# Late first reads, six first raw tiles and two closing banks on ScalarE in a two-layer decoder trunk

## The chip, the cores and the metric

The kernel runs on one core of a Trainium2 chip, as one program. The metric is the device time of one execution in microseconds (us). The core has TensorE (PE in the profile; PEld is its weight load), VectorE (DVE), ScalarE (ACT), GpSimd (POOL) and SyncE (SP), each with its own in-order queue. DMAs are issued here from SP's queue (q1 of the profile) and from POOL's (q0) and share 16 DMA engines.

## The reference: what is computed

Two layers over x (1, 256, 2048) in float32. The weights come from memory once per execution, in float32.

```python
h = rms_norm(x, attn_norm)
proj = einsum('bsd,de->bse', h, w_in)           # 2048 x 6160
# gated linear attention heads, stick-breaking heads, each normalised -> mixed
x = x + einsum('bse,ed->bsd', mixed, w_o)       # 2048 x 2048
hm = rms_norm(x, mlp_norm)
up = square(relu(einsum('bsd,df->bsf', hm, w_up)))   # 2048 x 8192
x = x + einsum('bsf,fd->bsd', up, w_down)       # 8192 x 2048
```

## The kernel before, in words

**Products.** Each float32 operand is split in a high part (rounded to TensorE's float32r) and a low part (the rest), and a product is three matmuls: high·high, high·low, low·high (L1224, L1227, L1228). For a weight tile, ScalarE makes the high part `whi` (L1091) and VectorE the low part `wlo` (L1095) from the loaded tile `raw`. `raw` tiles of 1 MB are loaded over SP's queue (L1016) into three slots (`RAWS`).

**Big units.** The large products are cut in units of 256 rows by 1024 columns over 2048 inputs: `up` and `down`, in four quarters of two units each, `o`, and, one layer ahead, `iv`, `ik` and `iq` of the next layer's input projection. A unit goes over eight pairs of 256 inputs, cut in 2 x 2 blocks. A fast pair takes seven block products instead of eight: VectorE forms four sums of weight blocks (`ts` and in place, L871) and four of operand blocks (`forms`, L464 to L467), and the products go to PSUM banks named m1 to m8. Banks m2, m4, m3, m8 are the four output blocks; m1, m6, m5, m7 are sums that the unit's closing distributes over them. Pairs that aren't fast go to the four output banks alone. Two pairs of each unit ("added") get their weights by POOL's queue instead: `chi` is loaded (L1052), ScalarE writes its negative into `dlo` (L1056), and a second, adding load (L1059) turns that into the low part. There are three `chi` tiles; in the first scope each of the first three loads comes behind a one-column ScalarE write into its tile (`held_tile`, L1045), which reads `ident`.

**Closing a unit.** `up_tail` (L1338) and `seeded_tail` (L1288) first copy m1 (ScalarE), then VectorE forms dw = m6 - m1 and adds: m5 + dw, m7 + dw, m5 + that; when an output bank is done, VectorE adds it, one addition for each of the four. A bank is free for the next unit when its last reader is done. Units that follow an `up` unit turn its output by TensorE transposes into m5 and m7 behind their first step, and into m1 and m6 behind their second (`turn`, L1384); units behind `o`, and (`down`, 3, 1) and `iv` in layer 0, do so with the residual.

**Order.** `Plan` takes each piece of work with an engine, an estimated length and what it depends on, simulates the engines, and writes the order of TensorE, VectorE and ScalarE out by hand (`manual_schedule`); of the ready pieces the one due first goes first. A unit's order of pairs stands in lists (`EACH`, `FEWER`, `LATER`, `O0`, `O1`, `OWN`). Every scope of units opens with five prelude pieces of 12 matmuls each, which stand for the unit that is still running. GpSimd's and SP's queues are ordered by the compiler, in which earlier lines go first among what is ready.

**Scopes.** The program opens with one plain unit (columns of `w_in`, lines L607 to L628, whose output is `acc`) while x is loaded, turned (L503) and split (L513, L519) and its squares summed (L560). Then come `iv`, `ik`, `iq` of layer 0 in the first planned scope; layer 0's attention; its planned scope (the gate unit, `o`, `up`, `down`, and layer 1's `iv`, `ik`, `iq`); layer 1's attention; and its planned scope, which ends the program with (`down`, 3, 1) and the store of x. L917 copies the plain unit's `acc` out. Between attention and planned scopes PSUM is laid out anew: attention has two `acc` tiles of two banks, then four single banks (L242); a planned scope has eight single banks in an order of their first use (L250):

```python
open_scope("psum", acc=2, ps=4)
order = (1, 6, 5, 7) if first else (5, 7, 1, 6)
unused.update((m, new_bank(m)) for m in (*order, 2, 4, 3, 8))
```

Of the kernel before, what the change touches and what calls it, by code (L numbers as in the profile page):

```python
# [14 lines left out]
ALU = mybir.AluOpType  # L15
# [7 lines left out]
EACH = [7, 7, 5, 2, 5, 5, 1, 1, 5, 4, 1, 1, 3, 3, 3, 3, 4, 6, 6, 2, 6, 6, 0, 0], FAST, (2, 4)  # L23
FEWER = [0, 0, 3, 2, 3, 3, 2, 3, 1, 1, 1, 7, 7, 1, 6, 6, 4, 6, 4, 6, 5, 5], (1, 3, 6), (2, 4)
LATER = [0, 0, 4, 1, 1, 1, 1, 3, 3, 4, 6, 6, 3, 6, 3, 6, 2, 5, 5, 5, 5, 2, 7, 7], FAST, (2, 4)
FAST_OF = {"sxh": (0, 1, 3, 5, 6), "sx": FAST}
TWO_WAYS = (("sxh", 0),)
O0 = [6, 6, 7, 4, 5, 4, 0, 0, 1, 0, 7, 0, 1, 1, 1, 5, 2, 2, 2, 2, 3, 3], (0, 1, 2), (5, 7)
O1 = [5, 7, 7, 0, 0, 0, 1, 0, 6, 1, 1, 2, 1, 2, 2, 2, 5, 3, 6, 3, 4, 4], (0, 1, 2), (5, 6)
SEEDED = (("down", 0), ("down", 1), ("o", 1))  # L30
SPARE = ()
OWN = {
    ("up", 0): ([4, 0, 0, 0, 0, 1, 1, 2, 1, 1, 6, 6, 2, 6, 6, 5, 5, 5, 5, 4, 3, 3, 3, 3, 7, 7], (0, 1, 3, 5, 6), (2, 4)),
    ("up", 0, 0): ([0, 0, 1, 1, 1, 4, 4, 1, 3, 3, 3, 6, 6, 3, 2, 6, 6, 5, 5, 5, 5, 2, 7, 7], FAST, (2, 4)),
    ("up", 1): ([0, 0, 3, 3, 3, 3, 2, 1, 1, 1, 2, 1, 5, 5, 5, 4, 6, 5, 6, 6, 6, 7, 4, 7], FAST, (2, 4)),
    ("down", 0): ([0, 0, 3, 3, 1, 2, 3, 3, 1, 1, 5, 1, 4, 5, 5, 5, 2, 6, 6, 6, 6, 7, 7, 4], FAST, (2, 4)),
    ("down", 1): ([0, 0, 5, 5, 4, 5, 5, 6, 6, 6, 4, 6, 3, 3, 3, 1, 2, 3, 1, 1, 1, 2, 7, 7], FAST, (2, 4)),
}
CAST, AHEAD_BY = 3, 1
RING, LOWS, ADDS, RAWS = 5, 4, 2, 3  # L40
# [21 lines left out]
class Plan:  # L62
# [8 lines left out]
    GAP = 0.06  # L71

# [18 lines left out]
    def run(self):  # L91
# [32 lines left out]
        while events:  # L124
# [9 lines left out]
            for e in free:  # L134
# [38 lines left out]
def trunk_kernel(  # L173
# [275 lines left out]
    def forms(op, i, t, tag):  # L449
# [9 lines left out]
        def sums():  # L459
            a11, a21, a12, a22 = (t[:, k, r * P : (r + 1) * P] for k in range(2) for r in range(2))  # L460
            n = 4 if keep else 3
            e.append(tmp("t2", [P, 512], bufs=T2)[:, : n * P].rearrange("p (k c) -> p k c", c=P))
            s = e[0][:, 3, :] if keep else a21
            nc.vector.tensor_tensor(e[0][:, 2, :], a21, a11, ALU.subtract)  # L464
            nc.vector.tensor_tensor(s, a21, a22, ALU.subtract)
            nc.vector.tensor_tensor(e[0][:, 0, :], a11, s, ALU.subtract)
            nc.vector.tensor_tensor(e[0][:, 1, :], a12, e[0][:, 0, :], ALU.subtract)  # L467
# [387 lines left out]
    def ordered(l, units, hT, rst, ug, gates_t, mixed=None, ons=None):  # L855
# [4 lines left out]
        open_scope("sbuf", mlp=1)  # L860
        hm = Operand()
# [4 lines left out]
        MM, TR, V2, V1, A2, A1 = 0.2268, 0.109, 1.15, 0.62, 1.06, 0.60  # L866
# [84 lines left out]
        def made(f, got, tag_fast, first):  # L951
# [3 lines left out]
            def part(k):  # L955
                if not box:
                    box.extend(f())
                box[k]()
# [44 lines left out]
        def load(u, i):  # L1003
# [4 lines left out]
            def fn():  # L1008
                if x % RAWS >= 3:
                    box.append(tmp("raw2", [P, 2, 1024], bufs=RAWS - 3))  # L1010
# [9 lines left out]
            if x >= RAWS:  # L1020
                piece.after = raws[x - RAWS]
# [13 lines left out]
        def rounded(u, j, s):  # L1035
# [9 lines left out]
            def held_tile():  # L1045
                box["h"] = tmp("chi", [P, 2, 512], F32R, bufs=CAST)
                nc.scalar.activation(box["h"][:, 0, :1], ident[:, :1], AF.Copy)
# [15 lines left out]
            if l < 0 and len(chi) < CAST:  # L1063
                first = add("ACT", 0.2, held_tile, before[0])
# [223 lines left out]
        def seeded_tail(u):  # L1288
# [18 lines left out]
            def sums(p):  # L1307
# [7 lines left out]
                d = vector(x22, bk(5), dw, b, p[5], seeds[8])  # L1315
                free.update({1: [c], 6: [w], 5: [a, d], 7: [b]})
# [615 lines left out]
```

## Time and profile before

| what | value |
|---|---|
| median of three runs | 2134.3 us (2134.24 to 2135.91) |
| profiled execution | 2134.41 us, span 2132.7 us |
| TensorE / VectorE / ScalarE / GpSimd busy | 99% / 90% / 68% / 13% |
| mean granted clock of TensorE | 0.999 |
| moved by DMA | 497.14 MB, mean 233 GB/s |
| first planned scope | 38.3 to 164.9 us |
| planned scope of layer 0 | 296.0 to 1199.8 us |
| planned scope of layer 1 | 1352.0 us to the end |

The three scope rows are the starts of the first product into a named bank and of the first that is none. A timeline row has start, length, engine, line, operation, tiles written<-read, shapes, count, and in brackets the engine's idle time before it with what ended that. Matmul lengths overlap: dense matmuls of 512 columns start every 0.227 us, and a gap in the starts is a stall. VectorE's lengths overlap a little too.

### The profile page before, as it was taken

What the parts mean: (1) busy time and instruction counts of PE and PEld (TensorE: products, weight loads), DVE (VectorE), ACT (ScalarE), POOL (GpSimd) and SP (SyncE); (2) the same over time, 40 slices, a digit from 0 to 9 for tenths busy, and PEclk for the clock granted to TensorE, in tenths of its full rate; (3) what the DMA queues carried; (4) which work ended last, traced back from release to release, by engine and by line L of the source; (5) the groups of instructions that cost most, each with busy time, mean ns of one, the idle gap of its engine ahead of it and who ended that gap; (6) DMA issues with size and microseconds to landing.
All of it is one profiled execution on the core that took longest, in us unless ns stands there. A gap on an engine that the chain in (4) does not pass through costs nothing.

```text
span 2132.7 us, 28217 instructions
## 1 busy us (share of the span) xinstructions
PE 2120.0 (99%) x10064; PEld 1763.6 (83%) x10064; DVE 1909.1 (90%) x2578; ACT 1452.1 (68%) x1940; POOL 276.4 (13%) x394
## 2 busy tenths in 40 slices
PE   8999999999999999999999999999999999999999
PEld 7888888888888888888888988888888888888887
DVE  5978779999999999999988896799999999999997
ACT  6657667676677677667766575677776776676774
POOL 1110001111111111111111100011112111111110
PEclk9999999999999999999999999999999999999999
DMA  8975358788988988988888644678889788889886
GB/s 257 259 227 174 115 176 242 223 255 243 271 245 244 268 245 245 283 244 234 250 261 245 192 138 138 213 217 244 264 241 272 234 262 256 240 246 273 242 245 200
DMA packets 157617, 497.14 MB, mean 233 GB/s; under 512 B 10682, under 2 KB 19458, under 8 KB 157476
## 3 DMA queue, kind: packets, MB, share of 16 engines
q1 hardware_dynamic: 100900, 319.16, 42.0%
q0 software_dynamic: 56576, 176.18, 36.9%
q8 instruction: 79, 1.29, 0.2%
q14 instruction: 62, 0.51, 0.1%
HBM read 493.20 MB, written 2.10 MB: 232 GB/s over the span
## 4 chain that ended last, share of the span: by engine, by line
PE 94%; DVE 3%; DMA 2%; ACT 1%; issue 1%; SPq 0%; ACTq 0%; DVEq 0%
PE acc L626 3%; PE acc L628 3%; PE acc L627 3%; DVE wlo L1095 1%; DMA xb<-in_x_dram 1%; DMA raw<-in_w_up_dram 1%; DMA raw<-in_w_in_dram 1%; PE ps L1869 0%; PE ps L1862 0%; DVE wlo L609 0%; PE ps L737 0%; PE ps L1819 0%; DVE ts L871 0%; PE ps L791 0%; PE ps L755 0%
## 5 line engine op out<-in xcount | busy, mean ns | idle before, releaser
L1095 DVE TENSOR_TENSOR wlo<-raw,whi 128x1024 fp32r<-128x1024 f32 (+1 forms) x689 | 744.0, 1089 | 86.2 <-ACT whi L1091 39.8
L1091 ACT ACTIVATE whi<-raw 128x1024 fp32r<-128x1024 f32 (+1 forms) x689 | 644.7, 950 | 185.8 <-DVE raw L871 67.6
L1056 ACT ACTIVATE dlo<-chi 128x1024 fp32r<-128x1024 f32 x168 | 177.6, 1057 | 117.7 <-DMA chi<-in_w_o_dram 5.1
L1091 ACT ACTIVATE whi<-ts 128x1024 fp32r<-128x1024 f32 x169 | 179.0, 1059 | 89.9 <-DVE ts L871 42.2
L871 DVE TENSOR_TENSOR ts<-raw 128x1024 f32<-128x1024 f32 x169 | 206.1, 1220 | 6.3 <-DMA raw<-in_w_o_dram 2.4
L1095 DVE TENSOR_TENSOR wlo<-ts,whi 128x1024 fp32r<-128x1024 f32 x169 | 206.1, 1220 | 4.1 <-ACT whi L1091 4.1
L626 PE MATMUL acc<-whi,act 128*128 128x512 f32 (+2 forms) x384 | 141.7, 369 | 1.6 <-ACT whi L607 1.6
L627 PE MATMUL acc<-wlo,act 128*128 128x512 f32 (+2 forms) x384 | 137.1, 357 | 0.2 <-DVE wlo L609 0.2
L628 PE MATMUL acc<-whi,act 128*128 128x512 f32 (+2 forms) x384 | 137.3, 358 | 0.0
L607 ACT ACTIVATE whi<-raw 128x1024 fp32r<-128x1024 f32 (+2 forms) x98 | 88.3, 906 | 69.2 <-PE acc L628 62.4
L609 DVE TENSOR_TENSOR wlo<-raw,whi 128x1024 fp32r<-128x1024 f32 (+2 forms) x98 | 100.3, 1030 | 32.5 <-ACT whi L607 32.3
L871 DVE TENSOR_TENSOR raw<-raw 128x512 f32<-128x512 f32 x169 | 116.2, 688 | 2.3
L871 DVE TENSOR_TENSOR raw<-ts,raw 128x512 f32<-128x512 f32 x169 | 115.8, 685 | 0.6
L1052 POOL DMA_DIRECT2D chi<-in_w_up_dram x64 | 38.0, 594 | 557.9 <-PE m__2856_13480 L1228 30.1
L1052 POOL DMA_DIRECT2D chi<-in_w_down_dram x64 | 38.8, 606 | 498.5 <-PE m__3324_15675 L1228 27.5
L1376 ACT ACTIVATE act<-act,st 128x512 f32<-128x512 f32 x88 | 60.2, 715 | 54.9 <-DVE act L871 54.9
L626 PEld LDWEIGHTS acc<-whi,act 128*128 128x128 f32 x384 | 72.6, 189 | 14.1 <-issue 3.4
L628 PEld LDWEIGHTS acc<-whi,act 128*128 128x128 f32 x384 | 72.7, 189 | 10.6
L627 PEld LDWEIGHTS acc<-wlo,act 128*128 128x128 f32 x384 | 72.8, 190 | 9.4 <-DVE wlo L609 0.5
L1059 POOL DMA_DIRECT2D dlo<-in_w_down_dram x64 | 60.1, 940 | 51.6 <-ACT dlo L1056 48.1
L1059 POOL DMA_DIRECT2D dlo<-in_w_up_dram x64 | 58.3, 912 | 55.9 <-ACT dlo L1056 53.6
L488 DVE TENSOR_TENSOR act<-t,act 128x512 fp32r<-128x512 f32 x92 | 62.7, 685 | 0.0
(4307 smaller groups left out, 5756.4 us busy)
## 6 DMA issues: line engine op xcount, KB each, us to landing
raw<-in_w_up_dram SPq DMA_DIRECT2D x96, 1024.0 KB, 7.4
raw<-in_w_down_dram SPq DMA_DIRECT2D x96, 1024.0 KB, 7.7
raw<-in_w_in_dram SPq DMA_DIRECT2D x72, 1024.0 KB, 5.7
chi<-in_w_up_dram POOLq DMA_DIRECT2D x64, 512.0 KB, 5.6
dlo<-in_w_up_dram POOLq DMA_DIRECT2D x64, 512.0 KB, 8.5
chi<-in_w_down_dram POOLq DMA_DIRECT2D x64, 512.0 KB, 5.6
dlo<-in_w_down_dram POOLq DMA_DIRECT2D x64, 512.0 KB, 8.5
raw<-in_w_o_dram SPq DMA_DIRECT2D x24, 1024.0 KB, 7.5
```

The lines of the kernel that those rows point to most:

```text
L488: nc.vector.tensor_tensor(d[:, :, 1, :], src, f32(d[:, :, 0, :]), ALU.subtract)
L607: newest["hi"] = nc.scalar.activation(h, r, AF.Copy).ins
L609: newest["lo"] = nc.vector.tensor_tensor(lo[:, q : q + step, :width], r, f32(h), ALU.subtract).ins
L626: nc.tensor.matmul(o, xh[:, sl], whi[:, j, :width], start=first, stop=False)
L627: nc.tensor.matmul(o, xh[:, sl], wlo[:, j, :width], start=False, stop=False)
L628: st["mm"] = nc.tensor.matmul(o, xl[:, sl], whi[:, j, :width], start=False, stop=last).ins
L871: nc.vector.tensor_tensor(dst, a, b, op)
L1052: nc.gpsimd.dma_start(flat("h"), src)
L1056: nc.scalar.activation(box["l"], f32(box["h"]), AF.Copy, scale=-1.0)
L1059: nc.gpsimd.dma_start(flat("l"), src, accum_op=ALU.add)
L1091: nc.scalar.activation(box["h"][:, :n], src(), AF.Copy)
L1095: nc.vector.tensor_tensor(box["l"][:, :n], src(), f32(box["h"][:, :n]), ALU.subtract)
```

## The change

It has three parts.

1. `held_tile` reads the low part of the last operand pair of x instead of `ident`, and doesn't wait for a prelude piece any more in the plan.
2. The first scope has six raw tiles instead of three; the three new ones are `raw2` tiles of the scope's own pool. The planner counts 0.12 us between two VectorE pieces of which one needs the other, the four sums of `forms` become four pieces, and estimated lengths of VectorE pieces are adjusted. One kept operand of the MLP moves to the pool of activations (`SPARE`).
3. In `up_tail` and `seeded_tail`, ScalarE copies banks m4 and m8 into the output block, and VectorE adds from there. m5's second addition moves behind the copy of m8, and dw is kept until both last additions are done.

The orders of the pairs are new in nearly all lists; how often each pair stands in a list, and which are fast or added, is as before.

```diff
-EACH = [7, 7, 5, 2, 5, 5, 1, 1, 5, 4, 1, 1, 3, 3, 3, 3, 4, 6, 6, 2, 6, 6, 0, 0], FAST, (2, 4)
+EACH = [0, 0, 1, 1, 1, 2, 7, 3, 3, 3, 3, 2, 5, 5, 5, 5, 4, 1, 6, 6, 6, 4, 6, 7], FAST, (2, 4)
...
-SPARE = ()
+SPARE = ("sxh",)
...
+FIRST_RAWS = 6
...
+    SAME = {"DVE": 0.12}
...
-                        at[u], free[e] + p.lag + (0.0 if u.engine == e else self.GAP)
+                        at[u], free[e] + p.lag + (self.SAME.get(e, 0.0) if u.engine == e else self.GAP)
...
+        slots = RAWS if l >= 0 else FIRST_RAWS
...
-        MM, TR, V2, V1, A2, A1 = 0.2268, 0.109, 1.15, 0.62, 1.06, 0.60
+        MM, TR, V2, V1, VS, A2, A1 = 0.2268, 0.109, 1.14, 0.61, 0.21, 1.06, 0.60
...
-                e = add("DVE", 1.25, lambda: part(0), first, take=1, sure=1 + got)
+                for k in range(4):
+                    kw = {} if k else dict(take=1, sure=1 + got)
+                    e = add("DVE", VS, lambda k=k: part(0, k), e, **kw)
...
-                nc.scalar.activation(box["h"][:, 0, :1], ident[:, :1], AF.Copy)
+                nc.scalar.activation(box["h"][:, 0, :1], f32(hT.t[7][:, 1, 1, :1]), AF.Copy)
...
-                first = add("ACT", 0.2, held_tile, before[0])
+                first = add("ACT", 0.2, held_tile)
...
-                b = vector(y(0, 1), bk(7), lambda: box["w"], w, a, p[7])
-                b.give = 1
-                d = vector(y(1, 1), bk(5), y(0, 1), b, p[5])
-                free.update({1: [c], 6: [w], 5: [a, d], 7: [b]})
-                box["s"] = (c, b, a, d)
+                b = vector(lambda: box["w"], bk(7), lambda: box["w"], w, a, p[7])
+                free.update({1: [c], 6: [w], 5: [a], 7: [b]})
+                box["s"] = (w, b, a, b)
...
+                    before = p[m]
+                    if tt:
+                        free[m] = before = [add(
+                            "ACT", A1,
+                            lambda m=m, h=h: nc.scalar.activation(
+                                box[h][:, 1, :], banks[m], AF.Copy
+                            ),
+                            before, box["c"],
+                        )]
+                    if m == 8:
+                        before = vector(y(1, 1), bk(5), y(1, 1), before, p[5])
+                        free[5] = free[5] + [before]
```

`seeded_tail` has the same edit with the residual's blocks in place of y.

More of the change, by code (lines that the diff above doesn't have):

```diff
@@ L1019, in load @@
             piece = add("SP", 2.9, fn, lag=LAND)
-            if x >= RAWS:
-                piece.after = raws[x - RAWS]
+            if x >= slots:
+                piece.after = raws[x - slots]
             raws.append(readers)
```

86 lines of the change are left out of this document (51 added, 35 removed).

## The prediction

> **What bounds the kernel now.** I read the page's busy shares, then the table by stretches, then the timelines of the stretches where TensorE is not dense.
>
> ```profile
> span 2132.7 us, 28217 instructions
> PE 2120.0 (99%) x10064; PEld 1763.6 (83%) x10064; DVE 1909.1 (90%) x2578; ACT 1452.1 (68%) x1940; POOL 276.4 (13%) x394
> ...
> 10.00:15.00 5.00, 4.51 (x12) 3.26 (x12) 2.77 (x5) 1.62 (x4) 0.00 (x0) 0.67 1.08 401
> 500.00:600.00 100.00, 100.00 (x442) 82.78 (x441) 94.66 (x115) 65.47 (x74) 17.20 (x22) 1.00 0.91 260
> 1900.00:2000.00 100.00, 100.00 (x443) 82.84 (x442) 91.92 (x108) 64.44 (x72) 16.91 (x22) 1.00 0.95 273
> ```
>
> In the last three rows the columns are the stretch, then busy time of PE, PEld, DVE, ACT and POOL, the granted clock, the DMA share and GB/s. In the big units TensorE has no gap (100.00 of 100), VectorE 5 to 8% idle, ScalarE 35%. The orders of the steps are permuted, but how many fast pairs, added pairs and products a unit has is unchanged, so TensorE's work is too. Inside the big units there is nothing to win; what the change moves lies at the opening, where scopes meet, and at the end.
>
> The profiled execution took 2134.4 us (its span and 1.7 around it), the three timed runs have their median at 2134.3: one number for this purpose. The sum is made on 2134.4.
>
> **Held reads, the opening.** The three first `chi` loads wait for a tiny ScalarE write that today needs only `ident`.
>
> ```profile
> 2.63 1.77 POOL L1052 DMA_DIRECT2D chi<-in_w_in_dram x3 [1.24 <-ACT chi L1047]
> ...
> q1 hardware_dynamic: 1048, 1.95, 58.2%
> q0 software_dynamic: 432, 1.57, 42.9%
> ...
> DMA packets 2173, 4.63 MB, mean 386 GB/s; under 512 B 131, under 2 KB 131, under 8 KB 2172
> ...
> 6.32 1.57 ACT L513 ACTIVATE act<-ps,gcol_a 128x256 fp32r<-128x256 f32 x4 [3.83 <-DVE gcol_a L345]
> 9.58 0.63 ACT L607 ACTIVATE whi<-raw 128x512 fp32r<-128x512 f32 x1 [1.69 <-DMA raw<-in_w_in_dram]
> ...
> 10.26 0.51 PE L626 MATMUL acc<-whi,act 128*128 128x512 f32 x1 [1.56 <-ACT whi L607]
> 16.05 1.09 PE L503 MATMUL ps<-ident,xb 128*128 128x128 f32 x8 [0.68 <-DMA xb<-in_x_dram]
> 20.11 1.09 PE L503 MATMUL ps<-ident,xb 128*128 128x128 f32 x8 [0.23 <-DMA xb<-in_x_dram]
> 20.96 0.47 PE L626 MATMUL acc<-whi,act 128*128 128x512 f32 x1
> ```
>
> The two queue rows are of 4 to 15 us: 1.57 MB of `chi` (q0) beside 1.95 MB of x and opening weights (q1), while ScalarE and TensorE wait for exactly those (rows of 9.58, 16.05, 20.11). The next row is 15 to 27 us, 386 GB/s without `chi`: 1.57 MB cost 4.1 us there. Without them the first weights find ScalarE free at 7.9, so the first product starts near 8.4 instead of 10.3; the first twelve products then go at VectorE's pace (four `wlo` of 0.69) to 11.5, the next x is turned by 12.4, and ScalarE (four copies, 1.6; two `whi`, 1.9) and VectorE (1.2) allow the second group near 16.2 instead of 20.96. The half clock of 10 to 15 us (0.67) follows the gap before 10.26 and should go with it; that is in the 16.2. Bounds: 1.9 (first product alone) to 5.0; I take **-4.7**. From 20 us on TensorE is dense, so the gain lasts to the unit's end (38.5, now 33.8).
>
> **Held reads, the scope behind.** This is the step that I expect to spoil it.
>
> ```profile
> 28.22 1.66 DVE L519 SCALAR_TENSOR_TENSOR act<-ps,gcol_a,act 128x256 fp32r<-128x256 f32 x4 [0.72 <-ACT act L513]
> 28.70:34.30 5.60, 5.60 (x27) 4.62 (x26) 4.61 (x10) 5.60 (x14) 0.00 (x0) 1.00 0.60 192
> 33.70 0.28 ACT L560 ACTIVATION_READ_ACCUMULATOR t<-xb 128x1 f32 x1
> 33.79 1.13 ACT L1091 ACTIVATE whi<-raw 128x1024 fp32r<-128x1024 f32 x1
> 38.49 0.60 ACT L917 ACTIVATE act<-acc 128x512 f32<-128x512 f32 x1 [3.57 <-PE acc L628]
> 38.99 1.05 ACT L1056 ACTIVATE dlo<-chi 128x1024 fp32r<-128x1024 f32 x1
> 40.41 1.06 ACT L1091 ACTIVATE whi<-raw 128x1024 fp32r<-128x1024 f32 x1
> ...
> 41.52 0.49 PE L1224 MATMUL m__82_434<-whi,act 128*128 128x512 f32 x1 [0.35 <-ACT whi L1091]
> 42.78 0.50 PE L1227 MATMUL m__82_434<-wlo,act 128*128 128x512 f32 x1 [0.77 <-DVE wlo L1095]
> ...
> chi<-in_w_in_dram POOLq DMA_DIRECT2D x11, 512.0 KB, 7.5
> ```
>
> ScalarE's order in this scope is written out by the planner. Today a held write waits for the first prelude piece (12 products, 2.7), so by the planner's clock `chi` lands at 11.1, after the first `whi` is ready at 9.96 (2.9 issue, 7.0 landing, 0.06): the order is `whi`, L917, `dlo`, and the rows show it. With that dependence gone the held writes stand at 0, the first `chi` lands at 8.32 and the second at 9.32, so ScalarE's order becomes held, `dlo`, `dlo`, `whi`, L917. ScalarE is in order: no `whi` before two `chi` have landed. But now `chi` is issued only after the last operand's low part (L519, 29.9) and, I think, behind ScalarE's own backlog (5.60 of 5.60 us busy from 28.7 to 34.3): the `whi` of 33.79 stood behind it too. Shifted by 4.7 that is 29.3, with the three writes 29.7. Landing takes 7.5 (the row of 0 to 130 us), the second 1 to 2 later: 37 to 39; one `dlo` and one `whi` of 0.95 each and the `wlo` of 1.14 give 40.3 to 42.2 for the first complete product, where TensorE is free at 33.8. Before, the scope started at 38.3 and lost 1.65 (0.51 and 1.03 by the starts ahead of the rows of 41.52 and 42.78, 0.11 behind): 39.9 in effect. So this stage ends 0.4 to 2.3 later than before, 1.0 the likeliest, and TensorE has idled over 4 us. The gap of 1.56 before 10.26 was followed by a granted clock of 0.67 over 5 us, 1.65 us lost; after a longer gap I add 1.6 (0 to 3.4). Stage sum **+2.6** (bounds +0.4 and +5.7), the opening's gain included.
>
> [...]
>
> **Six raw tiles, ScalarE copies: what they take away.**
>
> ```profile
> 123.47 1.22 DVE L871 TENSOR_TENSOR ts<-raw 128x1024 f32<-128x1024 f32 x1 [0.58 <-DMA raw<-in_w_in_dram]
> 124.62 0.68 DVE L871 TENSOR_TENSOR act<-m__157_811,act 128x512 f32<-128x512 f32 x1
> ...
> 125.36 0.50 PE L1224 MATMUL m__229_1148<-whi,act 128*128 128x512 f32 x1 [1.07 <-DVE act L871]
> ```
>
> VectorE waits for a raw tile, the closing addition of bank 4 stands behind it, and TensorE waits for that bank: 1.34 us by the starts. With three more tiles the raw lands earlier, and bank 4 is freed by ScalarE. I take **-1.3** (0 to -1.3).
>
> **ScalarE copies: what they add.** Per big unit two copies of 0.60 (row of 158.33 below), some 40 units, 48 us on an engine with 680 idle; VectorE keeps eight operations a unit. But bank 5 now gets its last reader behind the copy of bank 8, the unit's last product.
>
> ```profile
> 158.33 0.60 ACT L1347 ACTIVATE act<-m__246_1226 128x512 f32<-128x512 f32 x1 [3.64 <-PE m__246_1226 L1228]
> ...
> 162.18 0.69 DVE L871 TENSOR_TENSOR act<-m__241_1210,act 128x512 f32<-128x512 f32 x1
> 165.13 0.69 DVE L871 TENSOR_TENSOR act<-m__234_1171,act 128x512 f32<-128x512 f32 x1 [0.20 <-PE m__234_1171 L1228]
> ...
> 164.71 0.39 PE L1228 MATMUL m__234_1171<-whi,act 128*128 128x512 f32 x1
> 164.93 0.28 PE L626 MATMUL acc<-whi,act 128*128 128x272 f32 x1
> ```
>
> Where a scope ends, attention's first `acc` opens in the first two banks of the new pool, where m5 and m7 lay (`order`, L252). Today m5's last read is at 162.18, long before TensorE goes on at 164.93. After: the product ends at 165.10, copy to 165.74, addition of bank 5 from 165.80 to 166.49, TensorE at 166.55: 1.6 us of stall at the least, 2.9 behind one other ScalarE and one VectorE operation of 0.65. I take 1.9, twice (scope before layer 0, end of layer 0): **+3.8** (0 to 5.8; 0 if the placing is otherwise). Elsewhere bank 5 is next needed by the transposes 2.72 us (12 products) behind the unit's end: covered while both queues together hold under 1.1 us.
>
> The end of the kernel:
>
> ```profile
> 2120.58 0.69 DVE L871 TENSOR_TENSOR xb<-m__4033_18993,t 128x512 f32<-128x512 f32 x1
> 2121.30 0.69 DVE L871 TENSOR_TENSOR t<-m__4034_18997,t 128x512 f32<-128x512 f32 x1
> ...
> 2128.62 0.69 DVE L871 TENSOR_TENSOR xb<-m__4024_18956,xb 128x512 f32<-128x512 f32 x1 [0.67 <-PE m__4024_18956 L1228]
> ```
>
> Behind the last product stands one addition, then the store. After: a copy of 0.60, a hand-over of 0.06 and a second, dependent addition 0.72 behind the first (spacing of the rows of 2120.58 and 2121.30): **+1.4**, with nothing to hide it (1.3 to 1.5).
>
> [...]
>
> **Dependent steps counted, split sums, one tile from the act pool.** The same instructions, re-ordered; TensorE is dense over them, so nothing to gain. If VectorE, 92 to 95% busy in the rows above, came late with operands, TensorE would wait: 0 to +3, I take 0.
>
> **Sum:** 2134.4 + 2.6 - 1.3 + 3.8 + 1.4 = 2140.9, forecast 2141.
>
> **Rivals.**
> 1. *The held writes come early.* If ScalarE has one idle slot after 25.2 (29.9 less 4.7), the writes slip in ahead of the backlog and `chi` is issued 4 us sooner: landed at 33 and 35, first product complete at 37. Against 39.9 that is -3 instead of +2.6, 2135.3. For it: the three extra raw loads have no tile to wait for and may overtake the opening's last weights, which gives ScalarE such a slot. Against: 28.7 to 34.3 is dense today.
> 2. *Faster.* As in 1, and attention's first product doesn't wait for bank 5: 2134.4 - 3 (or -4.7, with the start's stall as before) - 1.3 + 1.4 gives 2131.5 or 2129.8, and 2129.5 with a little more than my take of the opening. For it only that the placing of banks is read from the code, not from a row. Against it: the end costs 1.4 in any case.
> 3. *Bank 5 late inside the layers.* About 20 places (up to up, up to down, o to up) need it 2.72 us behind a unit's end; the bare path is 1.6. From 1.1 us of queueing on it costs; at 0.3 us each, 6 us: 2147. Against: the addition of 165.13 starts 0.03 behind its product (164.71 and 0.39 long), so queues can be kept short there.
>
> **How the numbers follow.** The forecast 0.47, held writes early 0.30, faster 0.12, bank 5 late 0.11. A measurement here tells about 0.2%, 4.3 us, from no change. The forecast's own range is 2137 to 2144: slower in 0.37 of its 0.47. Rival 1 (2131 to 2138) is nearly all no change, 0.26, with 0.01 faster and 0.03 slower; rival 2 faster; rival 3 slower in 0.10. Faster 0.13, same 0.37, slower 0.50. Eight in ten reach from 2130, most of rival 2 left out, to 2147, half of rival 3.
>
> **What would show it.** No q0 traffic before 20 us, granted clock 1.00 in 10 to 15, opening unit over near 34 (opening). ScalarE with two L1056-type copies ahead of the first L1091-type one, TensorE idle over 4 us behind the opening unit, waiting for `whi` (scope). Attention's first product 1.6 to 2.9 behind the last product of bank 8, twice, released by VectorE (bank 5). A ScalarE copy and two additions behind the last product (end). No wait near 124. Wrong if ScalarE issues the held writes before its squares, or if the first `acc` follows without a gap; a dense TensorE in the big units that is not dense any more would be a cost that I priced at nothing.

## The result and the profile after

The changed kernel takes 2146.5 us (median of 4 runs, 2144.4 to 2151.9) against 2134.3 (2134.2 to 2135.9): ratio 1.0062 with the interval 1.0050 to 1.0074. It is slower by 12.3 us, about twice the 6.7 that I had forecast: near the upper edge of the wide range (2130 to 2147), and outside the forecast's own (2137 to 2144). Its profiled execution is its longest: 2151.9 us, span 2150.2.

The page after, its first rows:

```profile
span 2150.2 us, 28296 instructions
PE 2121.5 (99%) x10064; PEld 1765.5 (82%) x10064; DVE 1902.3 (88%) x2578; ACT 1490.5 (69%) x2020; POOL 274.5 (13%) x394
```

80 ScalarE instructions more, TensorE's and VectorE's counts the same. The table by stretches after (columns as in the prediction: stretch, busy time of PE, PEld, DVE, ACT, POOL, granted clock, DMA share, GB/s):

```profile
8.00:15.00 7.00, 6.38 (x31) 5.04 (x32) 4.99 (x12) 5.44 (x12) 0.00 (x0) 1.00 1.05 396
33.10:36.40 3.30, 0.59 (x3) 0.16 (x1) 0.00 (x0) 0.00 (x0) 0.00 (x0) 1.00 1.06 408
36.50:46.60 10.10, 4.19 (x9) 3.00 (x10) 4.68 (x6) 7.50 (x9) 1.77 (x2) 0.50 0.99 238
132.00:136.00 4.00, 4.00 (x12) 3.12 (x11) 4.00 (x6) 2.10 (x4) 0.00 (x0) 0.57 1.04 245
500.00:600.00 100.00, 100.00 (x451) 82.99 (x450) 93.74 (x116) 71.28 (x87) 16.65 (x21) 1.00 0.89 258
1210.70:1214.00 3.30, 0.97 (x6) 0.54 (x5) 2.80 (x6) 2.48 (x6) 0.00 (x0) 1.00 0.00 0
1214.10:1217.40 3.30, 3.30 (x17) 3.30 (x16) 2.82 (x8) 1.38 (x2) 0.00 (x0) 0.50 0.54 159
```

The half clock of 10 to 15 us is gone and the big units are as dense as before. Three places are new: 33 to 47, 126 to 136, 1210 to 1217, each a TensorE that idles and then runs at a granted clock of 0.50: by the trace's clock records for 10.24 us from 36.46, for 3.41 from 132.03 and for 3.41 from 1214.06. A half-clock window, in the expectations below, is 3.41 us of it.

Where the 17.5 us of the profiled pair went, by the starts of matmuls with the same number in both traces: the 100th starts 4.77 earlier (opening), the 200th 4.63 later (the scope's start, so +9.4), the 600th 8.82 later (+4.2: 5.2 lost from 120 to 134 us, 1.0 gained ahead of it), the 700th 10.57 (+1.75, end of the first scope), the 4900th 11.26 (+0.7 over layer 0), the 5700th 15.39 (+4.1, end of layer 0), the last 16.16 (+0.8), and the end of the span is 1.34 further behind it.

The scope's start, timeline after:

```profile
29.44 0.48 ACT L1054 ACTIVATE chi<-act 128x1 fp32r<-128x1 f32 x3
30.05 1.77 POOL L1059 DMA_DIRECT2D chi<-in_w_in_dram  x3 [28.66 <-ACT chi L1054]
37.42 1.06 ACT L1063 ACTIVATE dlo<-chi 128x1024 fp32r<-128x1024 f32 x1 [7.50 <-DMA chi<-in_w_in_dram]
39.89 1.06 ACT L1063 ACTIVATE dlo<-chi 128x1024 fp32r<-128x1024 f32 x1 [1.42 <-DMA chi<-in_w_in_dram]
40.85 1.04 ACT L1098 ACTIVATE whi<-raw 128x1024 fp32r<-128x1024 f32 x1
41.95 0.79 PE L1231 MATMUL m__86_446<-whi,act 128*128 128x512 f32 x1 [8.26 <-ACT whi L1098]
43.20 0.79 PE L1234 MATMUL m__86_446<-wlo,act 128*128 128x512 f32 x1 [0.47 <-DVE wlo L1102]
```

ScalarE's order is held, `dlo`, `dlo`, `whi`, as forecast; TensorE stands 8.26 us for a `whi` whose raw tile had long landed. The stop at 126, the two scope ends and the end of the kernel, timeline after:

```profile
126.66 0.39 PE L1235 MATMUL m__167_840<-whi,act 128*128 128x512 f32 x1
127.54 1.23 DVE L876 TENSOR_TENSOR ts<-raw 128x1024 f32<-128x1024 f32 x1 [7.42 <-DMA raw<-in_w_in_dram]
130.42 0.68 DVE L876 TENSOR_TENSOR act<-act,m__158_802 128x512 f32<-128x512 f32 x1
131.24 0.47 PE L1231 MATMUL m__230_1143<-whi,act 128*128 128x512 f32 x1 [4.20 <-DVE act L876]
...
173.53 0.39 PE L1235 MATMUL m__238_1179<-whi,act 128*128 128x512 f32 x1
174.03 0.58 ACT L1391 ACTIVATE act<-m__238_1179 128x512 f32<-128x512 f32 x1
174.64 0.69 DVE L876 TENSOR_TENSOR act<-m__242_1201,act 128x512 f32<-128x512 f32 x1
175.38 0.40 PE L630 MATMUL acc<-whi,act 128*128 128x272 f32 x1 [1.46 <-DVE act L876]
...
1210.81 0.39 PE L1235 MATMUL m__2245_10618<-whi,act 128*128 128x512 f32 x1
1212.18 0.58 ACT L1391 ACTIVATE act<-m__2245_10618 128x512 f32<-128x512 f32 x1
1212.79 0.69 DVE L876 TENSOR_TENSOR act<-m__2250_10655,act 128x512 f32<-128x512 f32 x1 [0.47 <-ACT act L1391]
1213.53 0.39 PE L630 MATMUL acc<-whi,act 128*128 128x272 f32 x1 [2.33 <-DVE act L876]
...
2144.36 0.39 PE L1235 MATMUL m__4027_19039<-whi,act 128*128 128x512 f32 x1
2144.78 0.60 ACT L1332 ACTIVATE xb<-m__4027_19039 128x512 f32<-128x512 f32 x1 [2.12 <-PE m__4027_19039 L1235]
2145.41 0.69 DVE L876 TENSOR_TENSOR xb<-m__4037_19093,xb 128x512 f32<-128x512 f32 x1 [1.30 <-ACT xb L1332]
2146.14 0.69 DVE L876 TENSOR_TENSOR xb<-xb,t 128x512 f32<-128x512 f32 x1
```

At 126, VectorE is in order and stands 7.42 us for a raw tile; the closing addition of an output bank (130.42) is behind it, and TensorE waits for that bank. At 173 and 1210 the chain is the forecast one: product, copy, bank 5's addition, first `acc`. By the starts less one matmul (0.227) the two stops are 1.63 and 2.50. At the end a copy and two additions stand behind the last product.

What SP's queue waited for from 60 to 131 us (total, times, longest, us), after:

```profile
SPq L1023 <- DVE wlo L1102: 42.9, 7, 21.7
```

and before:

```profile
SPq L1016 <- DVE wlo L1095: 56.2, 10, 13.0
```

The flight of the raw tiles that were loaded in that stretch, after:

```profile
DMA to landing us min/median/max: 7.1/11.7/15.0
```

and before:

```profile
DMA to landing us min/median/max: 8.5/10.0/11.3
```

With six slots SP ran ahead, then stood 21.7 us in one piece (82.8 to 104.6) on a slot whose tile was read late; before, its longest stand was 13.0. The load that VectorE waits for at 127.5 is the third after that stand, issued at 112.73 (the same view from 112 to 113.2 us, that load alone):

```profile
DMA to landing us min/median/max: 14.8/14.8/14.8
```

### The profile page after: what moved, and what is told of

Same layout as the page of the kernel before. It is cut to its first block, busy times and chain, and to the rows that moved or that the text cites. A ratio compares the mean times of both kernels' runs of the same rounds, so it can differ in the third digit from the quotient of the medians.

```text
span 2150.2 us, 28296 instructions
## 1 busy us (share of the span) xinstructions
PE 2121.5 (99%) x10064; PEld 1765.5 (82%) x10064; DVE 1902.3 (88%) x2578; ACT 1490.5 (69%) x2020; POOL 274.5 (13%) x394
## 4 chain that ended last, share of the span: by engine, by line
PE 89%; DMA 3%; ACT 3%; DVE 3%; issue 1%; POOL 0%; DVEq 0%; ACTq 0%
PE acc L630 3%; PE acc L632 3%; PE acc L631 3%; DMA raw<-in_w_down_dram 2%; DVE wlo L1102 1%; DMA raw<-in_w_in_dram 1%; ACT whi L611 0%; DMA raw<-in_w_o_dram 0%; ACT whi L1098 0%; DMA chi<-in_w_in_dram 0%; DVE wlo L613 0%; PE ps L1903 0%; PE ps L1896 0%; DVE ts L876 0%; PE ps L741 0%
## 5 line engine op out<-in xcount | busy, mean ns | idle before, releaser
L1102 DVE TENSOR_TENSOR wlo<-ts,whi 128x1024 fp32r<-128x1024 f32 x169 | 205.7, 1217 | 2.6 <-ACT whi L1098 1.4
L632 PEld LDWEIGHTS acc<-whi,act 128*128 128x128 f32 x384 | 73.1, 190 | 10.4
```

What stands on the lines that cost most here:

```text
L632: st["mm"] = nc.tensor.matmul(o, xl[:, sl], whi[:, j, :width], start=False, stop=last).ins
L1102: nc.vector.tensor_tensor(box["l"][:, :n], src(), f32(box["h"][:, :n]), ALU.subtract)
```

## The experiments

All runs of the study; "before" ran beside each set (2133.9 to 2134.5). "Piece 3" means held writes behind the third prelude piece. The ratios are estimates with a 95% interval, not quotients of the two medians (1.0057 for the changed kernel).

| run | what it is | median us | ratio to before, interval |
|---|---|---|---|
| changed | | 2146.5 | 1.0062 (1.0050 to 1.0074) |
| e1_raws3 | changed, three tiles in the first scope | no kernel came of it | |
| e2_ident | changed, held writes read `ident` | 2149.6 | 1.0068 (1.0056 to 1.0080) |
| e3_order | changed, held writes behind prelude piece 1 | 2141.0 | 1.0037 (1.0024 to 1.0050) |
| f3_readonly | before, late read alone | 2133.0 | 0.9996 (0.9987 to 1.0004) |
| f2_nocopy | changed without copies | 2141.1 | 1.0034 (1.0021 to 1.0047) |
| f4_late_nocopy | f2, held writes behind piece 3 | 2130.2 | 0.9982 (0.9973 to 0.9991) |
| g1_copies_alone | before, copies alone | 2144.4 | 1.0050 (1.0038 to 1.0063) |
| e4_banks | changed, banks (7, 1) first | 2142.8 | 1.0045 (1.0033 to 1.0057) |
| g2_swap57 | changed, piece 3, banks (7, 5) first | 2135.2 | 1.0006 (0.9997 to 1.0015) |
| h1_banks72 | changed, piece 3, banks (7, 2) first | 2131.1 | 0.9989 (0.9980 to 0.9998) |
| f1_oldeach | changed, old order and three tiles in the first scope | 2144.1 | 1.0046 (1.0034 to 1.0059) |
| g3_threeraws | f4, old order and three tiles there | 2135.2 | 1.0006 (0.9997 to 1.0015) |
| g4_early_nocopy | f2, held writes as before | 2137.5 | 1.0017 (1.0008 to 1.0026) |
| h2_firstscope | before, late read, piece 3, new order and six tiles in the first scope | 2132.1 | 0.9994 (0.9985 to 1.0002) |
| i1_banks3 | changed, piece 3, banks chosen for each scope | 2130.3 | 0.9983 (0.9974 to 0.9992) |
| i2_banks3_end | i1, last unit closed as before | 2129.0 | 0.9976 (0.9967 to 0.9985) |

### The held writes

```diff
-                nc.scalar.activation(box["h"][:, 0, :1], f32(hT.t[7][:, 1, 1, :1]), AF.Copy)
+                nc.scalar.activation(box["h"][:, 0, :1], ident[:, :1], AF.Copy)
```

> The changed kernel with the held writes reading ident again (they can run at 2 us); ScalarE's order stays the changed one: held, dlo, dlo, whi. Theory: late chi behind that order is what costs at the scope's start, and the late read is what gains at the opening. So the opening unit ends again 4.8 later (first product near 10.3, half clock in 10 to 15), and the 9.5 us that TensorE lost at the scope's start (8.42 and 1.03 of stops, three half-clock windows) go down to the 1.7 of the kernel before: net -4.6, about 2142. Rival: the opening's gain came from the order of SP's loads and not from the read: then the opening stays at 33.3 and only the start's loss goes, -8 to -9, 2138.

Measured 2149.6 (five runs at 2149 to 2152, the profiled one 2141.3): 3 slower where I expected 4.6 faster. Timeline of this run:

```profile
10.37 1.06 ACT L1063 ACTIVATE dlo<-chi 128x1024 fp32r<-128x1024 f32 x1 [7.87 <-DMA chi<-in_w_in_dram]
```

The edit did not do what I wanted. With `chi` early and no prelude piece to hold it, the first `dlo` went to fifth place on ScalarE and held the whole opening for 7.87 us of landing; the first product came at 13.45. So it doesn't undo the late read cleanly; g4, below, does so in f2. It shows the same mechanism in another place: an in-order ScalarE behind a `dlo` that waits for a load. Where the five longer executions lost another 8 us isn't seen, as only the short one was profiled.

```diff
-                first = add("ACT", 0.2, held_tile)
+                first = add("ACT", 0.2, held_tile, before[0])
```

> The changed kernel, held writes still read the late operand, but the planner places them behind the first prelude piece as before. ScalarE's written order becomes held, whi, whi, dlo, whi, dlo in place of held, dlo, dlo, whi. Theory: the stop of 8.4 at the scope's start is ScalarE's order alone; chi still lands at 37 to 40, but two whi are made ahead of it. First complete product at 34 to 35.5 in place of 43.0, no half clock from 36 to 47: -8 to -10, 2136.5 to 2138.5, with the opening's 4.8 kept. Rival: what counts is when chi lands; the stop moves to the third whi or to the added products and half of it stays: -3 to -5, 2141.5 to 2143.5.

Measured 2141.0, 5.5 less, its profiled execution 2135.8. What TensorE waited for in it (total, times, longest, us):

```profile
PE acc L630 <- DVE act L876: 3.8, 2, 2.3
PE m__230_1143 L1231 <- DVE act L876: 1.2, 1, 1.2
PE m__83_436 L1234 <- DVE wlo L1102: 0.8, 1, 0.8
PE m__83_436 L1231 <- ACT whi L1098: 0.6, 1, 0.6
```

The wait of 8.3 is 0.8 and 0.6 (with the restarts 2.4 us by the starts), though `chi` landed no earlier: ScalarE's order made it. The stops at the scope ends (3.8) are still there, as the forecast had allowed for. The median lies between the theory's range and the rival's; the profiled execution is the shortest of five, and what the other four (2140.6 to 2143.7, mean granted clock 0.998 against 1.000) lost besides isn't seen.

The same on the kernel before, and alone:

```diff
-                nc.scalar.activation(box["h"][:, 0, :1], ident[:, :1], AF.Copy)
+                nc.scalar.activation(box["h"][:, 0, :1], f32(hT.t[7][:, 1, 1, :1]), AF.Copy)
```

> The kernel before with one edit of the change alone: the held writes read the late operand in place of ident. The planner's dependence, three raw tiles, the old orders and closings stay, so ScalarE's order is held, whi, L917, dlo, L917, whi. Theory: the opening gains 4 to 4.8 as in the changed kernel; at the scope's start one step is ready at 34, the second whi stands behind a chi that lands at 37.3, so TensorE loses 3 to 4 there and 1 to 2 at the fourth step, which is an added pair whose dlo lands near 45, where it lost 1.65 before, perhaps a half-clock window of 1.6: 2133 to 2136, spread as before (under 3). Rival: the late chi loads are the whole loss whatever ScalarE's order: 2138 to 2141. Other rival: the opening's gain comes from SP's order of loads (the raw tile hoisted ahead of opening weights), which is not in this kernel: then it gains under 2 and the kernel is at 2137 to 2140.

Measured 2133.0, 1.0 less, no difference that can be told. By the matmuls' numbers the opening gained 3.9 and the scope's start took 3.8 back. Waits and stretches of this run:

```profile
PE m__82_434 L1224 <- ACT whi L1091: 2.8, 1, 2.8
```

```profile
41.30:44.50 3.20, 3.20 (x8) 2.53 (x9) 3.20 (x4) 2.56 (x4) 0.81 (x1) 0.50 0.90 179
```

So the opening's gain is the read's, not that of SP's order, and one `dlo` ahead of the second `whi` costs 2.8 and a half clock.

Both losses taken away (the copies are left out as in f2, below):

```diff
-                first = add("ACT", 0.2, held_tile)
+                first = add("ACT", 0.2, held_tile, before[2])
```

> The changed kernel without ScalarE's copies, and with the held writes placed behind the third prelude piece, so that ScalarE's order is held, then four whi, then the two dlo. Theory: the three parts add up. Against the run with held, whi, whi, dlo, whi, dlo (2141.0; its profiled execution 2135.8): -5.5 for the copies (1.63 + 2.50 + 1.34) and -2.4 for the stops of 0.72, 1.03 and 0.65 at 39.7 to 43.2. Median 2132 to 2134, the profiled execution near 2128 if the stop near 124 is small in it: faster than the kernel before by 0 to 2. Rival: the added product of tile 2, whose dlo is now made last, is late and TensorE loses 2 to 4 near 47: 2135 to 2138.

Measured 2130.2 (2129.7 to 2131.4), faster than before by 3.9 and better than the theory's 2132 to 2134. Against f2 (2141.1) this one argument is worth 10.9 us. ScalarE makes four `whi` ahead of the two `dlo`; 0.56, 0.98 and 0.78 are left at 41 to 46, and the mean granted clock is 1.000. The spread is 1.7 us, where the changed kernel's was 7.5.

### The copies

The third part of the change taken out of the changed kernel, and put alone into the kernel before:

```diff
+                d = vector(y(1, 1), bk(5), y(0, 1), b, p[5])
...
-                    if tt:
-                        free[m] = before = [add(
-                            "ACT", A1,
...
-                    if m == 8:
-                        before = vector(y(1, 1), bk(5), y(1, 1), before, p[5])
...
```

> The changed kernel without ScalarE's copies of banks 4 and 8: the closing additions as before, the rest as changed. Theory: the copies cost 1.63 and 2.50 at the two scope ends, about 1.5 of half clock behind the second and 1.34 at the end of the kernel, and win nothing inside the layers: -5.5 to -7, 2139.5 to 2141. Rival: they free banks 4 and 8 sooner and the orders of the steps are made for that; without them TensorE waits for VectorE inside the layers, some 40 units at 0.1: -1.5 to -3, 2143.5 to 2145.

Measured 2141.1, 5.5 less; no wait of an `acc` for VectorE is left, and no half clock at the scope ends.

> The kernel before with one part of the change alone: ScalarE copies banks 4 and 8 out, bank 5's second addition behind the copy of bank 8, as in the changed kernel; held reads, raw tiles and orders as before. Theory: the copies cost where a scope ends under attention's first acc (1.6 to 2.9 each), half a clock window (1.7) where such a stop lies inside one window of the throttle, and 1.34 at the end; inside the layers nothing: +5 to +8, 2139 to 2142, and a spread over 4 since the window is luck. Rival: with the old orders, which were not made for them, the copies make TensorE wait inside the layers too: over 2143.

Measured 2144.4, 10.4 more than before, over the theory and in the rival's range. Waits of TensorE in it:

```profile
PE acc L626 <- DVE act L871: 4.9, 2, 3.2
PE m__1140_5425 L1227 <- DMA dlo<-in_w_up_dram: 1.1, 1, 1.1
```

With the old orders the first stop is 3.40 by the starts, with a half-clock stretch behind it that costs 1.5, the second 1.81, the end 1.34: 8.05 of the 9.7 by which its profiled execution is longer. A wait of 1.1 for a `dlo` load is new in layer 0, and by the matmuls' numbers 1.3 are lost there. So the bank and the end are the larger part; what the copies cost inside the layers, h1 below bounds.

Is it the bank? PSUM's first two banks chosen otherwise:

```diff
-        order = (1, 6, 5, 7) if first else (5, 7, 1, 6)
+        order = (1, 6, 5, 7) if first else (7, 1, 5, 6)
```

> The changed kernel with the PSUM banks of the scopes before layer 0 and of layer 0 laid out as (7, 1, 5, 6, ...) in place of (5, 7, 1, 6, ...), so that attention's two acc tiles lie where banks 7 and 1 were. Theory: the stops of 1.63 and 2.50 behind bank 8's last product are the wait for bank 5's last addition alone, and the half-clock window behind the second (about 1.5) follows from it: both stops under 0.3, -4 to -5.5, 2141 to 2142.5. Rival: the new pool opens when the last bank is read, or the next tile (ps, in bank 5 now) waits in its place: the stops stay or come 1 to 2 us later, 2145 to 2147.

Measured 2142.8, 3.7 less. Both stops are gone, and one came (first row):

```profile
PE m__620_2931 L1231 <- ACT act L922: 2.3, 1, 2.3
...
PE m__230_1143 L1231 <- DVE act L876: 0.4, 1, 0.4
```

That is layer 0's gate unit, which opens with banks 1 and 6: bank 1 now lay under the last `acc`, which L922 had to copy out first. So neither theory nor rival: the stop went to the other end of the layer.

The second row is the stop at 126, which was 4.2 in the changed kernel. The first scope of this run is that of the changed kernel but for the places of its banks: its start is blocked as long (8.1), and SP's longest stand is 20.6 against 21.7. The load that VectorE waits for, issued at 112.15, landed sooner (the view of 111.5 to 112.6 us):

```profile
DMA to landing us min/median/max: 12.2/12.2/12.2
```

So neither the blocked start nor the long stand makes the stop by itself; it came with 2.6 us more of flight, and why the load flew longer no run shows.

```diff
-        order = (1, 6, 5, 7) if first else (5, 7, 1, 6)
+        order = (1, 6, 5, 7) if first else (7, 5, 1, 6)
...
+                first = add("ACT", 0.2, held_tile, before[2])
```

> The changed kernel, copies and all, with two edits: the held writes behind the third prelude piece (ScalarE: four whi ahead of the two dlo), and PSUM's first two banks swapped, (7, 5, 1, 6) for (5, 7, 1, 6), so that attention's first acc lies where bank 7 was and only its second one where bank 5 was. Theory: both losses are mended; bank 5's last addition is over before the second acc opens, and bank 1 and 6 lie where they lay, so the stop of 2.46 that the layout (7, 1, 5, 6) brought at the layer's start isn't there. Left against the run without copies (2130.2) is the 1.34 at the end: 2131 to 2132.5, spread under 3. Rival: the second acc opens at once and waits for bank 5: 2135 to 2139, with the spread of the copies.

Measured 2135.2, in the rival's range, but not by its way: the stops of 1.63 and 2.50 are unchanged, and it is still the first `acc` that waits. An `acc` tile spans two banks, so attention's first product waits for both; which of them is bank 5 is no matter. Then with neither of them bank 5, 1 or 6:

```diff
-        order = (1, 6, 5, 7) if first else (5, 7, 1, 6)
+        order = (1, 6, 5, 7, 2, 4, 3, 8) if first else (7, 2, 1, 6, 5, 4, 3, 8)
...
-                first = add("ACT", 0.2, held_tile)
+                first = add("ACT", 0.2, held_tile, before[2])
```

> The changed kernel, copies and all, with the held writes behind the third prelude piece and PSUM's first two banks (7, 2) in place of (5, 7). The run with (7, 5) changed nothing: attention's first acc is one tile over both first banks, so it waits for the later of the two. Bank 7 and bank 2 are both read well before bank 8's last product, and neither is needed first by a layer's opening unit (banks 1 and 6). Theory: the copies' whole cost behind the layers' ends is bank 5 under that tile; both stops (1.63 and 2.50) go and no new one comes, and 1.34 at the end of the kernel is left against the run without copies (2130.2): 2131 to 2132.5, spread under 3. Rival: the copies cost inside the layers as well, as 10.4 against stops of 6.6 with the old orders hint: 2133 to 2136.

Measured 2131.1, in the theory's range, and both stops are gone; but a new one came, and the spread is 5.6 where I expected under 3. Timeline and waits of this run:

```profile
158.84 0.39 PE L1235 MATMUL m__238_1179<-whi,act 128*128 128x512 f32 x1
159.07 0.28 PE L630 MATMUL acc<-whi,act 128*128 128x272 f32 x1
...
1193.86 0.39 PE L1235 MATMUL m__2245_10618<-whi,act 128*128 128x512 f32 x1
1194.09 0.28 PE L630 MATMUL acc<-whi,act 128*128 128x272 f32 x1
```

```profile
PE m__80_433 L1231 <- ACT act L922: 2.1, 1, 2.1
```

`acc` follows bank 8's product at the dense pace of 0.23 with all 80 copies in place: within what these runs can tell, the copies cost nothing inside the layers. The new wait of 2.1 is bank 2 under the opening unit's `acc`, needed first in that scope.

### The first scope: six tiles and their order

The direct test, three tiles under the new order (e1_raws3), gave no kernel: that order holds more tiles open at once than three slots give. So tiles and order go back together:

```diff
-EACH = [0, 0, 1, 1, 1, 2, 7, 3, 3, 3, 3, 2, 5, 5, 5, 5, 4, 1, 6, 6, 6, 4, 6, 7], FAST, (2, 4)
+EACH = [7, 7, 5, 2, 5, 5, 1, 1, 5, 4, 1, 1, 3, 3, 3, 3, 4, 6, 6, 2, 6, 6, 0, 0], FAST, (2, 4)
-FIRST_RAWS = 6
+FIRST_RAWS = 3
```

> The changed kernel with the step order of the first scope's units (EACH) and its raw tiles (FIRST_RAWS = 3) as before; the rest as changed. The two go together: with three tiles the new order can't be planned, since it holds more tiles open at once. The changed kernel stood 4.36 us at 126.7 in its profile, 0.46 to 1.32 there in three variants, and its runs spread over 7.5 us where those of the kernel before spread over 1.8. Theory: six tiles with the new order make both. SP fills six slots by 82, then stands 22 us on a tile whose last reader comes late, and the loads behind it land in a burst. With the old order and three tiles: a stop under 1.4 near 124, -3 to -6 on the median, 2140.5 to 2143.5, spread under 3. Rival: the spread is the throttle's luck behind the stops of 8.4, 1.6 and 2.5, which all stay: median 2145 to 2148, spread still over 5.

Measured 2144.1 (2141.9 to 2144.7): 2.4 less, spread 2.8. No stop near 124 in its profile, but the stop behind the first scope is 3.40 here and pays a half-clock stretch. SP's longest stand is 12.8 here and its raw tiles fly 9.8 at most. The spread falls as the theory had it, the median by less.

> The run with late held writes and without copies (2130.2), with the first scope's step order and its three raw tiles as before. Tells what the six tiles and their order are worth once nothing else disturbs. Theory: the old order has the added pair of tile 2 at its fourth step; its dlo lands near 46 and TensorE would be there at 42, so 2 to 4 are lost at the start, and the stop near 120 falls from 1.7 to under 1.4: 2131.5 to 2134. Rival: six tiles only crowd the loads: 2128 to 2130. Other rival: no difference, 2130 to 2131.

Measured 2135.2, 5.0 more than f4, by the theory's way and over its range (2131.5 to 2134). TensorE's waits:

```profile
PE m__81_432 L1234 <- DMA dlo<-in_w_in_dram: 4.4, 1, 4.4
```

With late held writes the old order asks for tile 2's `dlo` 4.4 us before it has landed; the new one, which has tile 2 two steps later, doesn't. So with late held writes order and tiles are worth 5.0 together; which of the two, no run tells.

The held writes as before, in f2:

```diff
-                nc.scalar.activation(box["h"][:, 0, :1], f32(hT.t[7][:, 1, 1, :1]), AF.Copy)
+                nc.scalar.activation(box["h"][:, 0, :1], ident[:, :1], AF.Copy)
...
-                first = add("ACT", 0.2, held_tile)
+                first = add("ACT", 0.2, held_tile, before[0])
```

> The changed kernel without copies, with the held writes as in the kernel before (they read ident and the planner has them behind the first prelude piece, so no dlo slips into the opening, as it did in the run with ident alone, whose first dlo stood fifth on ScalarE from 2.5 us and held the opening until 11.3). Against 2130.2 (late read, no copies) this gives the worth of the late read alone, in the changed surroundings. Theory: the opening ends 4.3 later, and the stops of 0.56, 0.98 and 0.78 at 41 to 46 are gone: +2, 2131.5 to 2133. Rival: the raw tile that SP now loads ahead of the last opening weights makes the crowded opening worse than in the kernel before: 2134 to 2137. Other rival: the late read is worth nothing here: 2129.5 to 2130.5.

Measured 2137.5, 7.3 above f4 and over every range that I gave: the late read, with the place of its writes in the plan, is worth more in these surroundings than the 2 that I expected. Waits:

```profile
PE m__232_1155 L1231 <- DVE act L876: 3.5, 1, 3.5
PE acc L630 <- ACT whi L611: 3.2, 1, 3.2
PE m__229_1141 L1231 <- DVE act L876: 1.8, 1, 1.8
```

The opening waits 3.2 for its first weights, and the stop of 122 to 126 is here too, 3.5 and 1.8. So that stop isn't a matter of the blocked start alone: it is 4.2 in the changed kernel, where the start is blocked for 8.3, and 0.4 in e4, where it is blocked for 8.1; 1.2 in e3, 1.5 in f4, 2.2 in h2, none in g2, h1, i1 and i2. In the changed kernel and e4 it goes with the flight of one load; what sets that flight, no run singles out.

Only the first scope changed, layers and closings as before:

```diff
+FIRST_RAWS = 6
...
-                nc.scalar.activation(box["h"][:, 0, :1], ident[:, :1], AF.Copy)
+                nc.scalar.activation(box["h"][:, 0, :1], f32(hT.t[7][:, 1, 1, :1]), AF.Copy)
...
-                first = add("ACT", 0.2, held_tile, before[0])
+                first = add("ACT", 0.2, held_tile, before[2])
```

> The kernel before with three edits, all at the first scope: the late read, the held writes behind the third prelude piece, and the changed step order of that scope's units with six raw tiles. Dependent steps are not counted, sums not split, no tile from the act pool, no copies, and the step orders of the layers as before. Theory: nothing of the change outside the first scope is worth anything, so this is the run without copies again: 2129.5 to 2131. Rival: the orders of the layers and the counted steps are worth 1 to 3 by themselves: 2131.5 to 2133.5, or, if they cost, 2127 to 2129.

Measured 2132.1 (2130.0 to 2136.9), in the rival's range; its interval and f4's overlap. The rival's reason isn't seen: between the 600th and the last matmul it gains 0.6 us on the kernel before and f4 loses 0.6, both under what a measurement can tell (4.3), so counted steps and layer orders are worth nothing that shows. In its profile it waits 2.2 at 120 and 1.6 at 45, in the first scope, against 1.5 and 0.6 in f4.

### A version faster than both

```diff
-        order = (1, 6, 5, 7) if first else (5, 7, 1, 6)
+        order = (7, 2, 1, 6, 5, 4, 3, 8) if first else (1, 6, 5, 7, 2, 4, 3, 8)
...
-                mlp_psum(l > 0)
+                mlp_psum(l == 0)
...
-                first = add("ACT", 0.2, held_tile)
+                first = add("ACT", 0.2, held_tile, before[2])
```

> The changed kernel, copies and all, held writes behind the third prelude piece, and PSUM's first two banks chosen for each scope: (1, 6) before layer 0, (7, 2) in layer 0, (1, 6) in layer 1 as before. With (7, 2) everywhere TensorE stood 2.28 at the first scope's start, since its first step uses banks 2 and 3 and bank 2 lay under the opening unit's acc. Theory: that stop goes and the two scope ends stay free: against 2131.1, -2 to -2.5, 2128.5 to 2129.2. Rival: the start is then held by the dlo copies and their low parts at 41 to 46, as in the run without copies (0.56, 0.98 and 0.78 there against 0.46): -0 to -1, 2130 to 2131.

Measured 2130.3: the rival was right. The stop of 2.28 is gone, and 0.58, 0.98 and 0.62 by the late `dlo` stand at 41 to 46 instead.

```diff
+                last_unit = kind == "down" and q == 3 and n2 == 1 and l + 1 == DEPTH
+                seeds, *tails[u] = (plain_tail if last_unit else seeded_tail)(u)
```

(`plain_tail` is `seeded_tail` of the kernel before.)

> The same, with the closing of the very last unit as in the kernel before: no copies there, one addition behind the last product. Theory: the 1.34 between the last product's start and the end of the span comes back, 2127 to 2128, the fastest so far. Rival: VectorE has the additions of both banks to do at the end and gives half of it away: 2128 to 2128.7.

Measured 2129.0 (2128.3 to 2129.6), over both ranges, which were reckoned from a lower i1. It is 1.2 less than i1; the intervals of the two overlap, and the traces have the end 1.36 nearer to the last product. It is 5.1 faster than before (0.9976, 0.9967 to 0.9985) and 17.5 faster than the change as it stood, with the late read, the six tiles, the new orders and all copies but one unit's kept. What differs is the place of the held writes in the plan and the banks.

## Why the prediction was half right

- **Opening, -4.7:** -4.8. No half clock, first product at 8.4, the gain held to the unit's end. f3 has 3.9 of it on the old kernel.
- **The scope behind, +2.6 with the opening in it:** +4.6 in the profile, inside its bounds (0.4 to 5.7). The mechanism is as it was put, mis-sized at two terms. The second `chi` landed 2.5 behind the first, not 1 to 2, so the first complete product came at 43.2, not 40.3 to 42.2. The half clock of 36.5 to 46.6 cost 1.2, of 1.6 charged (the 9.4 lost there, and the 1.65 lost there before, less the stops of 8.42, 1.03 and 0.36). f4 shows what I had not seen: the loss was in the order alone, and the same reads with the `whi` first would have kept most of the opening's gain.
- **Six tiles and copies, -1.3 at 124: this step failed, in its sign.** The wait that I called removed was 4.2 us in the profiled execution, with a half clock behind it, and my bounds (0 to -1.3) had no room for a loss. I counted slots and not the queue: with six, SP runs ahead, then stands 21.7 on the first slot that is read late, and the load that VectorE needs behind it took 14.8 to land. The stand alone isn't the cause: e4 has one of 20.6, and with a flight of 12.2 it waits 0.4. Why the load flew longer stays open. And the three more tiles helped in no run here: the wait of 1.1 of the kernel before is gone with the copies alone (g1) and in the other runs with three tiles and the changed plan (f1, g3); with six tiles it is gone where copies and late held writes are both in (g2, h1, i1, i2), and without copies it is 1.5 to 3.5 (f4, h2, f2, g4).
- **Bank 5 at the scope ends, +3.8:** shown by h1, in which both stops go with the banks. In the changed kernel stops of 1.63 and 2.50, 4.1 together, and f2 puts the copies at 5.5 against 5.2 for this and the end. The step was right in place and in chain. What it left out is the clock: behind the second stop TensorE ran 3.4 us at 0.50, which cost 1.6.
- **End, +1.4:** 1.34 by the rows, 1.2 by i2.
- **Dense layers, 0:** held within what can be told (h2; 1.5 in small waits in the changed kernel), as did the belief that bank 5 isn't late inside the layers (h1).
- **Rivals.** Held writes came behind the squares, so rival 1 fell; the first `acc` waited, so rival 2 fell; rival 3 fell with the dense layers.

The sum (2140.9) was short by 5.6 us of the median and by 11.0 of the profiled execution. By the latter's matmuls: 2.0 at the start (4.6 against 2.6), 5.5 from the 200th matmul to the 600th (4.2 against -1.3), 2.1 at the two scope ends (1.75 and 4.1 against 3.8), 1.5 in small ones inside the layers. The median's share of the stop at 126 isn't known: only one execution of the changed kernel was profiled.

## What to carry to other kernels

When a load is made later, look at what stands behind its first reader on an in-order engine: a copy that waits for the load must come after all work that doesn't (TensorE stood 8.26 us here), and one argument to a planner can be worth more (10.9 us) than the change it belongs to. When a closing step moves to the end of a chain, ask not only who reuses that bank next but how many banks the next tile spans. And more buffers can let a queue run ahead until it stands on the one that is read last (21.7 us here with six, 13.0 with three), so count how long it stands there, and not only the buffers.

## What the runs showed of the hardware

A stop can cost more than its length. The changed kernel's stop of 2.50 at 1210.8 was followed by a granted clock of 0.50 for 3.41 us, with TensorE busy for 0.97 us of the 3.30 ahead of it (rows above); g2's stop of the same 2.50, at the same place of the program, was not:

```profile
1195.30:1198.10 2.80, 0.46 (x3) 0.09 (x1) 2.30 (x6) 2.36 (x6) 0.00 (x0) 1.00 0.00 0
1198.20:1201.50 3.30, 3.30 (x28) 3.30 (x27) 3.20 (x8) 1.45 (x3) 0.00 (x0) 1.00 0.49 127
```

Two more runs divide the same way. Behind e4's stop of 2.46 the matmuls went from 0.40 and 0.42 us to 0.62 and 0.63, from 303.35 on. Behind e3's, a wait of 2.3 as in g2, none followed: the mean granted clock of its profiled execution is 1.000, and 3.41 us at 0.50 would have made it 0.999. So of these four stops of 2.5, all in profiled executions, two were followed by a half clock, which cost 1.6 in the changed kernel, and two were not. What decides it, no run singles out.

The half clock came in pieces of 3.41 and of 10.24 us, three times that, in the changed kernel, and of 3.41 (from 11.66) in the kernel before. In the changed kernel the second and the third piece start 95.57 and 1177.60 us after the first, 28 and 345 times a third of 10.24. My estimate from these starts and lengths is that in this execution the granted clock changed only at points 3.41 us apart. g1's expectation charges half a window, 1.7, where a stop lies inside one window: no run shows that condition. What g1 showed is a stretch behind its stop of 3.40 that cost 1.5.

The spread fits the stops too. The kernels in which stops of 1.6 to 3.7 us stand (changed, e2 to e4, f1 to f3, g1, g2, g4, h1, h2) spread over 2.8 to 10.3 us; f4, i1 and i2, with none over 1.7, over 1.2 to 1.7; and g3, whose longest stop is 4.55, over 1.8. It is argued from the sizes of the stops, not shown for each execution, and the smallest of these spreads don't stand out: the kernel before, whose longest stop is 1.6, spreads over 1.8 to 2.6.
